# Spatial-gating statistics in two rounds with a bias table, and expert gate and up matrices laid out by tile

## The chip, the core and the metric

One core of a Trainium2 chip runs the whole program. The metric is the device time of one execution in microseconds; runs of the same kernel are compared by their median. TensorE is called PE, VectorE DVE, ScalarE ACT, GpSimd POOL and SyncE SP, as in the profile. DMAs to and from DRAM are issued by SP (plain ones) and by POOL (indirect ones); all share 16 DMA engines.

## The reference

One transformer layer on 2048 tokens of width 1024, in float32. A joint projection gives q, k, v (512 columns each) and u, vs (512 each). Attention works on a 32 x 64 grid with an 8 x 16 window. Beside it stands a spatial gating unit, which is what the first part of the change is about:

```python
def spatial_gating(u, vs, ln_g, ln_b, w_s, b_s):        # u, vs already through gelu
    n_chunks = T // SGU_CHUNK                            # chunks of 128 tokens
    vg = vs.reshape(B, T, SGU_GROUPS, SGU_GROUP_DIM)     # 8 groups of 64 channels
    vg = layer_norm(vg, ln_g, ln_b)                      # over the 64 channels of a group
    vg = vg.reshape(B, n_chunks, SGU_CHUNK, SGU_GROUPS, SGU_GROUP_DIM)
    mixed = jnp.einsum('gpq,bnqgd->bnpgd', w_s, vg) + jnp.transpose(b_s)[:, :, None]
    return u * mixed.reshape(B, T, D_SGU)
```

The two outputs are normalized, joined, projected, added to x and layer-normed. Then comes a mixture of 16 SwiGLU experts (4 groups of 4; each token goes to the best group and to two experts in it), which is what the second part is about:

```python
for e in range(MOE_EXPERTS):                             # D_EXPERT = 256
    act = jax.nn.silu(hf @ w_gate[e]) * (hf @ w_up[e])   # w_gate[e], w_up[e]: 1024 x 256
    y = y + combine[:, e:e + 1] * (act @ w_down[e])      # w_down[e]: 256 x 1024
```

A second residual and layer norm end the layer.

## The kernel before

Nearly every matrix product is made of three fp32r passes: each operand is split into a high part (a cast on ACT) and a remainder (a subtraction on DVE). The helper `split` issues the two, the helper `passes` issues the three matmuls (L132 to L134). So a matmul needs ACT and DVE to have split its operands, and these need the loads. Every line number of a split is L142 (ACT) or L143 (DVE); the tile's name tells which it is.

Four stages follow each other, with overlap at the seams. `phase_a` (to about 420 us) makes the projection and the gating unit. `phase_b` makes attention, output projection, first layer norm and routing. Its end runs together with the first experts (`Moe.ahead`, `Moe.early`). `Moe.main` works off the remaining expert jobs. A tail normalizes the last tokens.

The order of instructions on PE, ACT, DVE and POOL is the order in which the program writes them; nothing reorders them afterwards. SP's DMAs are put in order by the framework, and each engine waits with semaphores for what it reads and for buffers to come free.

`phase_a` is a sequence of blocks, `block(h, col, ...)`, one for a half of the tokens `h` and a group of 512 columns `col`. For half 0 the order is v (col 2), vs (4), k (1), u (3), q (0). For half 1 it is q, vs, u, k. A block has two sets of 4 accumulators (the first block of all: 6 and 2); for each of 8 slices of the contraction a set issues 4 x 3 matmuls of 512 columns, and then calls `pipe.step()`. At a set's end a generator (`fin_vs`, `fin_k`, ...) starts to finish the results. The pipe advances every live generator by one `yield` a step, so that a `yield` in a generator means "after the next 12 big matmuls".

`fin_vs` finishes four tiles `g` of vs, 128 tokens x 512 channels each. Counted in steps from the set's end: at 0 gelu and the sums `su`; at 1 subtraction of the mean and the sum of squares, tile by tile, with DVE and ACT in turn; at 2 the power -1/2 on POOL (tile `r`); from 4 to 7, one tile a step, the product with `r` on DVE and, on POOL, the product with the gain `gb` and the sum with the shift `bb`; at 11 the split into `vh` and `vl`; at 13 and 14 the mixing matmuls, four groups of 2 x 3 matmuls of 256 columns into PSUM tiles `mx` (two buffers), with ACT and DVE adding the bias `bs` on the way to the tile `mt`; at 15 `mt` goes to DRAM (`md`). `fin_u` reads `md` back later.

The tile `mt` has one buffer. `fin_k` uses the same buffer for half of its results, and writes them to DRAM (`kd`); the next user waits for that DMA. `fin_k` of half 0 uses two `kt` tiles first and then the two halves of `mt`. `load_sgu` loads and splits the mixing matrices `wsT` once, at the start.

The MoE works in jobs of one expert each. `load_gu(j, f)` loads a quarter of a job's gate and up matrices: a 1024 x 128 piece, 512 KB, to a tile [128 x 8 x 128] of a ring of four tiles `wr`, then splits it to `wh` and `wl`. `load_d` does it with `w_down` (rows of 4 KB) through the same ring. In DRAM an expert's gate matrix is 1024 x 256, so the piece consists of 1024 runs of 512 B. Two small jobs of the leading experts (those with `lo` above 0) load halves, two 256 KB DMAs for a tile, whose rows of 512 B lie alternately in the tile. `down` scales the result on ACT (`y`) and adds it to the tokens' rows in DRAM by an indirect DMA with accumulation (`xad<-y`, issued by POOL). `gather` fetches rows (`xg<-x1d`).

Of the kernel before, what the change touches and what calls it, by code (L numbers as in the profile page):

```python
# [8 lines left out]
F32 = mybir.dt.float32  # L9
F32R = mybir.dt.float32r  # L10
I32 = mybir.dt.int32
AF = mybir.ActivationFunctionType
OP = mybir.AluOpType
# [4 lines left out]
P = 128  # L18
T = 2048
D = 1024  # L20
KC = D // P
# [6 lines left out]
E = 16  # L28
# [12 lines left out]
NVT = 12  # L41
PSTART = 21
LATE = 14
YA = 3
YB = 2
YG = 0
FIRST = 256
WARM = 8
# [47 lines left out]
def pool(c, es, name, bufs, side="left", psum=False):  # L96
    if psum:
        return es.enter_context(c.tc.tile_pool(name=name, bufs=bufs, space=PSUM, reuse_waits="tile"))
    return es.enter_context(c.tc.tile_pool(name=name, bufs=bufs, side=side, reuse_waits="tile"))
# [37 lines left out]
def bcast(ap, n):  # L137
    return bass.AP(tensor=ap.tensor, offset=ap.offset, ap=[[0, P], [1, n]])


def split(nc, hi, lo, src):
    nc.scalar.copy(hi, src)  # L142
    nc.vector.tensor_tensor(lo, src, hi.bitcast(F32), op=OP.subtract)  # L143


def phase_a(c, xT, w_in, wsT, bsT, sg_g, sg_b):
    tc, nc = c.tc, c.nc
# [7 lines left out]
    with ExitStack() as es:  # L155
# [3 lines left out]
        sp = pool(c, es, "sp", 1, "right")  # L159
        ev = pool(c, es, "ev", 2, "right")  # L160
        acc = pool(c, es, "acc", 6, psum=True)
        mx = pool(c, es, "mx", 2, psum=True)
# [40 lines left out]
        gb = sp.tile([P, 512], F32, name="gb")  # L203
        bb = sp.tile([P, 512], F32, name="bb")
        bs = sp.tile([P, 8], F32, name="bs")
# [4 lines left out]
        def load_sgu():  # L210
            nt, ng = 3 * E * S // P, 8 * T // P
            z = sp.tile([P, nt + ng], I32, name="mt")
            zt, zg = z[:, 0:nt].rearrange("p (r o) -> p r o", o=3), z[:, nt:].rearrange("p (r o) -> p r o", o=2)
            nc.vector.memset(z, 0)
            for v in (zt, zg):
                nc.vector.memset(v[:, :, 1:2], NONE)
            nc.vector.memset(zg[:, :, 0:1], T)
            nc.sync.dma_start(c.table[:, :].rearrange("(p c) o -> p c o", p=P), zt)
            nc.sync.dma_start(c.gtok[:, :].rearrange("(p c) o -> p c o", p=P), zg)
            nc.sync.dma_start(gb, bcast(sg_g, 512))  # L220
            nc.sync.dma_start(bb, bcast(sg_b, 512))
            nc.sync.dma_start(bs, bsT)
            wsr = sp.tile([P, 8, P], F32, name="mt")
            nc.sync.dma_start(wsr, wsT)
            yield
            yield
            split(nc, wsh[:, :, :], wsl[:, :, :], wsr[:, :, :])
            yield pipe

        def fin_v(h, units, ps):  # L230
# [10 lines left out]
        def fin_vs(h, units, ps):  # L241
            q = (h * 8 + units[0]) // 4
            g = [ev.tile([P, 8, 64], F32, name="g", bufs=8) for _ in range(4)]
            su = ev.tile([P, 4, 8], F32, name="su")
            for n in range(4):
                nc.scalar.activation(g[n], ps[n], AF.Gelu_apprx_tanh)
                nc.vector.tensor_reduce(su[:, n], g[n], axis=AX.X, op=OP.add)
            yield
            va = ev.tile([P, 4, 8], F32, name="va")
            for n in range(4):  # L250
                nc.vector.scalar_tensor_tensor(g[n], su[:, n, :, None].to_broadcast([P, 8, 64]), -1.0 / 64, g[n],
                                               op0=OP.mult, op1=OP.add)
                sq = ev.tile([P, 8, 64], F32, name="sq")
                nc.scalar.activation(sq, g[n], AF.Square)
                nc.vector.tensor_reduce(va[:, n], sq, axis=AX.X, op=OP.add)
            nc.vector.tensor_scalar(va, va, 1.0 / 64, EPS, op0=OP.mult, op1=OP.add)  # L256
            yield
            r = ev.tile([P, 4, 8], F32, name="r")
            nc.gpsimd.tensor_tensor(r, va, mhalf[:, :, :], op=OP.pow)  # L259
            yield  # L260
            yield
            vh = sp.tile([P, 4, 512], F32R, name="vh")
            vl = sp.tile([P, 4, 512], F32R, name="vl")
            for n in range(4):
                nc.vector.tensor_tensor(g[n], g[n], r[:, n, :, None].to_broadcast([P, 8, 64]), op=OP.mult)
                f = g[n][:, :, :].rearrange("p a d -> p (a d)")
                nc.gpsimd.tensor_tensor(f, f, gb, op=OP.mult)
                nc.gpsimd.tensor_tensor(f, f, bb, op=OP.add)
                yield
            for _ in range(YA):  # L270
                yield
            for n in range(4):
                f = g[n][:, :, :].rearrange("p a d -> p (a d)")
                split(nc, vh[:, n, :], vl[:, n, :], f)
            for _ in range(YB):
                yield
            mt = sp.tile([P, 4, 512], F32, name="mt")
            for g2 in range(4):
                pm = mx.tile([P, 2, 4, 64], F32, name="mx")
                for j in range(2):  # L280
                    e = g2 * 2 + j
                    s = slice(e * 64, (e + 1) * 64)
                    passes(nc, pm[:, j], wsh[:, e, :], wsl[:, e, :], vh[:, :, s], vl[:, :, s], True, True)
                for j in range(2):
                    e = g2 * 2 + j
                    s = slice(e * 64, (e + 1) * 64)
                    if j:
                        nc.vector.tensor_scalar(mt[:, :, s], pm[:, j], bs[:, e:e + 1], None, op0=OP.add)
                    else:
                        nc.scalar.activation(mt[:, :, s], pm[:, j], AF.Identity, bias=bs[:, e:e + 1])  # L290
                if g2 % 2 or YG:
                    yield
            for n in range(4):
                nc.sync.dma_start(md[q * 4 + n], mt[:, n, :])
            yield pipe
# [113 lines left out]
        x, w = [], []  # L409
# [9 lines left out]
        w, _ = block(0, 2, x, w, 4, first=True)  # L419
        w, _ = block(0, 4, x, w, 1)  # L420
        w, _ = block(0, 1, x, w, 3)
        w, _ = block(0, 3, x, w, 0)
        _, x = block(0, 0, x, w, None, nxt_x=1)
        w, _ = block(1, 0, x, w, 4)
        w, _ = block(1, 4, x, w, 3)
        w, _ = block(1, 3, x, w, 1)
        w, _ = block(1, 1, x, w, 2)
# [556 lines left out]
class Moe:  # L984
# [56 lines left out]
    def load_gu(self, pipe, j, f, lag=1):  # L1041
        nc = self.c.nc
        pos, lo, _ = JOBS[j]
        whole = j in G32
        h = self.wp.tile([P, KC, P], F32R, name="wh")
        if whole:
            r = h[:, :, :].bitcast(F32)
        else:
            r = self.raw()[:, :].rearrange("p (k f) -> p k f", k=KC)
            l = self.wp.tile([P, KC, P], F32R, name="wl")  # L1050
        m, q = divmod(f, 2)
        s = slice(m * P, (m + 1) * P)
        e = bass.ds(self.ex[pos], 1)
        if lo:
            r4 = r.rearrange("p (k o) f -> p k o f", o=2)
            for i in range(2):
                src = self.w[i][e, q * 512:(q + 1) * 512, s]
                nc.sync.dma_start(r4[:, :, i], src.rearrange("o (k p) f -> (o p) k f", p=P))
        else:
            self.issued = nc.sync.dma_start(r, self.w[q][e, :, s].rearrange("o (k p) f -> (o p) k f", p=P)).ins.name  # L1060
        self.gw[j, f] = (r, None) if whole else (h, l)
        if whole:
            return

        def rest():
            for _ in range(lag):
                yield
            split(nc, h[:, :, :], l[:, :, :], r)
            yield pipe
        pipe.add(rest())  # L1070
# [215 lines left out]
    def main(self):  # L1286
        c, tc, nc = self.c, self.c.tc, self.c.nc
        es, xg, out = self.es, self.xg, self.out
        w_gate, w_up, w_down = self.w
# [257 lines left out]
        def over(mi, i):  # L1547
            e = nc.values_load(mi[0:1, bass.ds(1 + i, 1)], engines=SP, min_val=0, max_val=E - 1)
# [4 lines left out]
            for q, w in enumerate((w_gate, w_up)):  # L1553
                t = self.xp[0].tile([P, KC, W], F32R, name=("xh", "xl")[q])
                f = t[:, :, 0:FF].bitcast(F32)
                nc.sync.dma_start(f, w[bass.ds(e, 1)].rearrange("o (k p) f -> (o p) k f", p=P))
                wts.append(f)
            wd = self.xp[1].tile([P, 2, D], F32, name="xh")
            nc.sync.dma_start(wd, w_down[bass.ds(e, 1)].rearrange("o (k p) d -> (o p) k d", p=P))
# [5 lines left out]
            for h in range(2):  # L1565
                pt = ps.tile([P, 4, P], F32, name="tp")
                for k in range(4):
                    q = (h * 4 + k) * P
# [28 lines left out]
        for j in range(2, nj):  # L1597
# [4 lines left out]
            for u in range(4):  # L1602
# [4 lines left out]
                if 4 * j + u in (LN2, LN2 + 1):  # L1607
                    r = nc.sync.dma_start(*((lng, bcast(self.ln2g, D)), (lnb, bcast(self.ln2b, D)))[4 * j + u - LN2])
# [10 lines left out]
                jn, f = divmod(4 * j + u + 5, 4)  # L1619
                if jn < nj and jn > 2:  # L1620
                    self.load_gu(pipe, jn, f, LAG)
                jn, f = divmod(4 * j + u + 1, 4)
# [7 lines left out]
                if todo and u in (CU if j < nj - 3 else CT):  # L1630
                    g, i = todo.pop(0)
# [48 lines left out]
    return mid.transpose(1, 0, 2), edge  # L1680


# [32 lines left out]
```

## Time and profile before

| | |
|---|---|
| median of 3 runs | 1328.71 us (1328.42 to 1332.13) |
| the profiled execution | 1326.6 us, its span 1324.9 us |
| mean granted PE clock | 0.972 |
| PE busy | 1230.7 us of the span |
| DVE, ACT, POOL busy | 775.6, 576.1, 452.4 us |
| moved by DMA | 261.73 MB in 193506 packets, mean 198 GB/s |

In the profile an instruction is named by its line, its engine and the tiles, output first (`mx<-vh,wsh`). "A <- B: 7.1, 2, 3.7" in a view of waits means that A waited for B 7.1 us in all, 2 times, 3.7 us the longest. In the timeline the columns are start, duration, engine, line, operation, count, and in brackets the idle time of the engine before it and what ended it. In a table of stages the last three numbers are the granted clock, the mean busy share of the 16 DMA engines (which can read a little over 1), and the GB/s that they moved. PE is busy nearly all the time, so that what the span loses is to be sought in the stretches where PE waits, or where its clock is low.

### The profile page before, as it was taken

The page shows a single profiled execution, that of the slowest core. Times are in us where ns is not written, and L with a number is a line of the kernel's source. Part 1 is how long each engine was busy: PE and PEld are TensorE (multiplying, and loading weights), DVE is VectorE, ACT ScalarE, POOL GpSimd, SP SyncE. Part 2 cuts the span into 40 slices and gives each one's busy share as a digit, 9 for nine tenths or more (in the row PEclk, how much of TensorE's full clock was granted, in tenths as well). Part 3 has the DMA queues.
Part 4 walks back from the last instruction along what each step waited for, and adds up shares of the span by engine and source line. Part 5 has one row for each costly group of instructions (what it writes and reads, how often), then busy time and mean ns, then how long its engine had stood idle before and what let it go on. Part 6 is the DMA issues. An engine that isn't in the chain of part 4 may idle for free. (4 is left out here: it accounts for less than half of the span.)

```text
span 1324.9 us, 22205 instructions
## 1 busy us (share of the span) xinstructions
PE 1230.7 (93%) x7932; PEld 1048.7 (79%) x7932; DVE 775.6 (59%) x1622; ACT 576.1 (43%) x1218; POOL 452.4 (34%) x448
## 2 busy tenths in 40 slices
PE   9998999999899997999999999988888999998980
PEld 7886888888788775888888888768777999998970
DVE  5358233424853226576676676876466568777655
ACT  5324233322342236545545445334466555555522
POOL 0046000003710013234435434442323357565475
PEclk9998999999899997999999999999999999999995
DMA  8602634450254689578668676372999999999984
GB/s 253 199 24 97 229 120 164 161 189 18 89 182 167 180 257 289 170 187 199 166 187 196 160 219 194 97 227 76 257 277 301 250 270 287 297 293 306 280 250 137
DMA packets 193506, 261.73 MB, mean 198 GB/s; under 512 B 51120, under 2 KB 126128, under 8 KB 193392
## 3 DMA queue, kind: packets, MB, share of 16 engines
q1 hardware_dynamic: 175408, 204.88, 51.6%
q0 software_dynamic: 17984, 55.40, 14.9%
q8 instruction: 63, 1.03, 0.3%
q14 instruction: 51, 0.42, 0.1%
HBM read 184.17 MB, written 80.24 MB: 200 GB/s over the span
## 5 line engine op out<-in xcount | busy, mean ns | idle before, releaser
L143 DVE TENSOR_TENSOR wl<-wr,wh 128x512 fp32r<-128x512 f32 (+1 forms) x132 | 139.4, 1063 | 96.8 <-ACT wh L142 95.6
L618 POOL TENSOR_SCALAR lg<-lg,s 128x352 f32<-128x352 f32 (+3 forms) x128 | 80.2, 626 | 289.6 <-DVE s L617 226.4
L142 ACT CAST wh<-wr 128x512 fp32r<-128x512 f32 (+1 forms) x132 | 109.6, 843 | 85.0 <-DMA wr<-w_in 41.1
L132 PE MATMUL acc<-wh,xh 128*128 128x512 f32 x320 | 125.9, 393 | 0.1
L133 PE MATMUL acc<-wl,xh 128*128 128x512 f32 x320 | 125.3, 392 | 0.2 <-DVE wl L143 0.2
L134 PE MATMUL acc<-wh,xl 128*128 128x512 f32 x320 | 125.3, 391 | 0.2
L132 PE MATMUL gu<-xh,wh 128*128 128x256 f32 (+2 forms) x416 | 124.5, 299 | 0.0
L134 PE MATMUL gu<-xh,wl 128*128 128x256 f32 (+2 forms) x416 | 124.0, 298 | 0.0
L133 PE MATMUL gu<-xl,wh 128*128 128x256 f32 (+2 forms) x416 | 123.9, 298 | 0.0
L132 PE MATMUL acc<-xh,wh 128*128 128x512 f32 x256 | 101.0, 395 | 0.7 <-DVE kt L143 0.7
L134 PE MATMUL acc<-xh,wl 128*128 128x512 f32 x256 | 100.3, 392 | 0.0
L133 PE MATMUL acc<-xl,wh 128*128 128x512 f32 x256 | 100.2, 391 | 0.0
L633 ACT COPY pT<-pt 128x384 f32<-128x384 f32 (+3 forms) x128 | 57.7, 451 | 97.4 <-PE pt L631 95.3
L605 DVE CUSTOM_DVE_ANT_0 lg<-l,tm 128x352 f32<-128x352 f32 (+3 forms) x128 | 57.8, 452 | 70.6 <-PE l L134 45.2
L259 POOL TENSOR_TENSOR r<-va,mhalf 128x32 f32<-128x32 f32 x4 | 22.5, 5636 | 212.3 <-DVE va L256 212.3
L1227 POOL DMA_INDIRECT xad<-y,ix x38 | 64.7, 1704 | 54.4 <-ACT y L1206 31.6
L1112 POOL DMA_INDIRECT xg<-x1d,ix x40 | 48.1, 1203 | 101.8 <-PE tp L1131 37.0
L132 PEld LDWEIGHTS gu<-xh,wh 128*128 128x128 f32 x416 | 79.5, 191 | 1.4
L133 PEld LDWEIGHTS gu<-xl,wh 128*128 128x128 f32 x416 | 79.2, 190 | 1.3
L134 PEld LDWEIGHTS gu<-xh,wl 128*128 128x128 f32 x416 | 79.1, 190 | 0.0
L134 PEld LDWEIGHTS acc<-wh,xl 128*128 128x128 f32 x320 | 60.3, 189 | 13.7 <-DVE xl L143 1.1
L133 PEld LDWEIGHTS acc<-wl,xh 128*128 128x128 f32 x320 | 60.4, 189 | 13.2 <-DVE wl L143 0.9
(325 smaller groups left out, 3230.2 us busy)
## 6 DMA issues: line engine op xcount, KB each, us to landing
wr<-w_in SPq DMA_DIRECT2D x72, 256.0 KB
wr<-w_down SPq DMA_DIRECT2D x34, 512.0 KB
kt<-kd SPq DMA_DIRECT2D x24, 704.0 KB
wr<-w_gate SPq DMA_DIRECT2D x30, 512.0 KB
wr<-w_up SPq DMA_DIRECT2D x30, 512.0 KB
sd<-kt SPq DMA_DIRECT2D x16, 512.0 KB
qb<-qd SPq DMA_DIRECT2D x64, 128.0 KB
sr<-sd SPq DMA_DIRECT2D x16, 512.0 KB
```

The lines of the kernel that those rows point to most:

```text
L132: nc.tensor.matmul(out, lhsT=ahi, rhs=bhi, start=first, stop=False)
L133: nc.tensor.matmul(out, lhsT=ahi, rhs=blo, start=False, stop=False)
L134: nc.tensor.matmul(out, lhsT=alo, rhs=bhi, start=False, stop=last)
L142: nc.scalar.copy(hi, src)
L143: nc.vector.tensor_tensor(lo, src, hi.bitcast(F32), op=OP.subtract)
L259: nc.gpsimd.tensor_tensor(r, va, mhalf[:, :, :], op=OP.pow)
L605: nc.vector.tensor_tensor_reduce(out=l[:, :N], in0=o.rearrange("p r c -> p (r c)"), in1=bias, scale=-1.0, scalar=3.0e38, op0=OP.add, op1=O ...
L618: nc.gpsimd.tensor_scalar(l[:, :N], l[:, :N], s, 1.0, op0=OP.mult, op1=OP.mult)
L633: nc.scalar.copy(w[0:n, 0:len(ch)], pt[0:n, 0:len(ch)])
L1112: nc.gpsimd.indirect_dma_start(out=self.xg[(self.slot[j] + s) % NXG][0:m, :], out_offset=None, in_=c.x1d[0:rows, :], in_offset=bass.Indire ...
L1227: return self.c.nc.gpsimd.indirect_dma_start(out=self.c.xad[0:rows, :], out_offset=bass.IndirectOffsetOnAxis(ap=ix, axis=0), in_=y, in_off ...
```

## The change

In `fin_vs`: the four subtractions of the mean are issued first, and then the four pairs of square and sum (two rounds). The power on POOL follows in the same step. The product with the gain `gb` moves from POOL to DVE, ahead of the product with `r`. The sum with `bb` leaves this place: since the mixing is linear, the shift enters the result as (row sum of the mixing matrix) x shift, and `load_sgu` turns `bb` into a table of that plus `bs`, once, with 8 matmuls against a column of ones and 8 operations on DVE. `mt` is then written by DVE alone, one addition of the table for each PSUM tile, where before it took two instructions, one each on ACT and DVE. Two constants of the order change: YA goes, YB becomes 4. Counted in steps: squares and power at 1, gain at 2, product with `r` and split at 5, mixing matmuls at 9 and 10, `mt` to DRAM at 11.

In the MoE: the host lays the gate and up matrices out as [expert, half of the columns, 128 rows, 8, 128], so that each of the 128 partitions of a 512 KB load reads one run of 4 KB. For the halves of the small jobs a partition reads one run of 2 KB, and the tile still receives rows of 512 B. The number of these DMAs and their order stay. A rarely taken path (`over`) follows the layout.

```diff
 def load_sgu():
     ...
             split(nc, wsh[:, :, :], wsl[:, :, :], wsr[:, :, :])
+            for _ in range(8):
+                yield
+            pr = mx.tile([P, 8], F32, name="mx")
+            for e in range(8):
+                nc.tensor.matmul(pr[:, e:e + 1], lhsT=wsr[:, e], rhs=c.ones, start=True, stop=True)
+            rs = sp.tile([P, 8], F32, name="rs")
+            nc.vector.tensor_copy(rs, pr)
+            for e in range(8):
+                s = slice(e * 64, (e + 1) * 64)
+                nc.vector.tensor_scalar(bb[:, s], bb[:, s], rs[:, e:e + 1], bs[:, e:e + 1], op0=OP.mult, op1=OP.add)
 def fin_vs(h, units, ps):
     ...
                 nc.vector.scalar_tensor_tensor(g[n], su[:, n, :, None].to_broadcast([P, 8, 64]), -1.0 / 64, g[n],
                                                op0=OP.mult, op1=OP.add)
+            for n in range(4):
                 sq = ev.tile([P, 8, 64], F32, name="sq")
                 nc.scalar.activation(sq, g[n], AF.Square)
                 nc.vector.tensor_reduce(va[:, n], sq, axis=AX.X, op=OP.add)
             nc.vector.tensor_scalar(va, va, 1.0 / 64, EPS, op0=OP.mult, op1=OP.add)
-            yield
             r = ev.tile([P, 4, 8], F32, name="r")
             nc.gpsimd.tensor_tensor(r, va, mhalf[:, :, :], op=OP.pow)
+            yield
+            for n in range(4):
+                f = g[n][:, :, :].rearrange("p a d -> p (a d)")
+                nc.vector.tensor_tensor(f, f, gb, op=OP.mult)
+            yield
             yield
             yield
     ...
                 nc.vector.tensor_tensor(g[n], g[n], r[:, n, :, None].to_broadcast([P, 8, 64]), op=OP.mult)
                 f = g[n][:, :, :].rearrange("p a d -> p (a d)")
-                nc.gpsimd.tensor_tensor(f, f, gb, op=OP.mult)
-                nc.gpsimd.tensor_tensor(f, f, bb, op=OP.add)
-                yield
-            for _ in range(YA):
-                yield
+                nc.scalar.copy(vh[:, n, :], f)
             for n in range(4):
                 f = g[n][:, :, :].rearrange("p a d -> p (a d)")
-                split(nc, vh[:, n, :], vl[:, n, :], f)
+                nc.vector.tensor_tensor(vl[:, n, :], f, vh[:, n, :].bitcast(F32), op=OP.subtract)
             for _ in range(YB):
                 yield
     ...
-                    if j:
-                        nc.vector.tensor_scalar(mt[:, :, s], pm[:, j], bs[:, e:e + 1], None, op0=OP.add)
-                    else:
-                        nc.scalar.activation(mt[:, :, s], pm[:, j], AF.Identity, bias=bs[:, e:e + 1])
+                add = bb[:, s].rearrange("p (j d) -> p j d", j=2)[:, :, None, :].to_broadcast([P, 2, 4, 64])
+                nc.vector.tensor_tensor(mt[:, :, s].rearrange("p n (j d) -> p j n d", j=2), pm, add, op=OP.add)
 def load_gu(self, pipe, j, f, lag=1):
     ...
-                src = self.w[i][e, q * 512:(q + 1) * 512, s]
-                nc.sync.dma_start(r4[:, :, i], src.rearrange("o (k p) f -> (o p) k f", p=P))
+                src = self.w[i][e, m, :, q * 4:(q + 1) * 4, :]
+                nc.sync.dma_start(r4[:, :, i], src.rearrange("o p k f -> (o p) k f"))
         else:
-            self.issued = nc.sync.dma_start(r, self.w[q][e, :, s].rearrange("o (k p) f -> (o p) k f", p=P)).ins.name
+            self.issued = nc.sync.dma_start(r, self.w[q][e, m].rearrange("o p k f -> (o p) k f")).ins.name
+def by_tile(w):
+    return w.reshape(E, KC, P, 2, P).transpose(0, 3, 2, 1, 4)
```

How the instructions stand on DVE, half 0, from the statistics of the second vs set on (`su` to `va`; `vl` here is still that of the first set), before:

```order
L247 TENSOR_REDUCE su<-g 128x8 x4
L251 SCALAR_TENSOR_TENSOR g<-su,g 128x512
L255 TENSOR_REDUCE va<-sq 128x8
L251 SCALAR_TENSOR_TENSOR g<-su,g 128x512
L255 TENSOR_REDUCE va<-sq 128x8
L251 SCALAR_TENSOR_TENSOR g<-su,g 128x512
L255 TENSOR_REDUCE va<-sq 128x8
L251 SCALAR_TENSOR_TENSOR g<-su,g 128x512
L255 TENSOR_REDUCE va<-sq 128x8
L256 TENSOR_SCALAR va<-va 128x32
L143 TENSOR_TENSOR vl<-g,vh 128x512 x4
```

And the same engine now, from the gain of the first set (L272) to the power's input of the second (L266):

```order
L272 TENSOR_TENSOR g<-g,gb 128x512 x4
L142 TENSOR_TENSOR wl<-wr,wh 128x512
L279 TENSOR_TENSOR g<-g,r 128x512 x4
L284 TENSOR_TENSOR vl<-g,vh 128x512 x4
L142 TENSOR_TENSOR wl<-wr,wh 128x512 x3
L256 TENSOR_REDUCE su<-g 128x8 x4
L296 TENSOR_TENSOR mt<-mx,bb 128x2x4x64 x2
L260 SCALAR_TENSOR_TENSOR g<-su,g 128x512 x4
L265 TENSOR_REDUCE va<-sq 128x8 x4
L266 TENSOR_SCALAR va<-va 128x32
```

The first set's `vl` moved from behind the second set's statistics to before them.

The second place is where `fin_k` of half 0 has filled `mt` and the second vs set wants it for its mixing result. DVE before:

```order
L143 TENSOR_TENSOR kt<-acc,kt 128x512 x2
L143 TENSOR_TENSOR mt<-acc,mt 128x512 x2
L143 TENSOR_TENSOR vl<-g,vh 128x512 x4
L143 TENSOR_TENSOR wl<-wr,wh 128x512
L288 TENSOR_SCALAR mt<-mx,bs 128x4x64 x2
L143 TENSOR_TENSOR wl<-wr,wh 128x512
L288 TENSOR_SCALAR mt<-mx,bs 128x4x64 x2
```

DVE now:

```order
L284 TENSOR_TENSOR vl<-g,vh 128x512 x4
L142 TENSOR_TENSOR wl<-wr,wh 128x512 x3
L142 TENSOR_TENSOR kt<-acc,kt 128x512 x2
L142 TENSOR_TENSOR mt<-acc,mt 128x512 x2
L296 TENSOR_TENSOR mt<-mx,bb 128x2x4x64 x4
L142 TENSOR_TENSOR wl<-wr,wh 128x512 x4
```

The write of `mt` by the mixing results now follows directly on `fin_k`'s write of `mt`; on PE its matmuls stand one step (12 big matmuls) behind the end of `fin_k`'s set, where it was five. SP's queue at that place, now:

```order
L308 DMA m<-md_140 128x512
L189 DMA wr<-w_in 128x512 x3
L349 DMA kd_129<-kt 256x1x512 x2
L349 DMA kd_130<-mt 256x1x512 x2
L300 DMA md_141<-mt 128x512
L300 DMA md_142<-mt 128x512
```

Before, the four loads of `m` stood behind the four writes of `kd`, and one load of `wr` ahead of them; now the loads of `m` and three loads of `wr` stand ahead.

More of the change, by code (lines that the diff above doesn't have):

```diff
@@ L43 @@
 LATE = 14
-YA = 3
-YB = 2
+YB = 4
 YG = 0
@@ L283, in fin_vs @@
                     passes(nc, pm[:, j], wsh[:, e, :], wsl[:, e, :], vh[:, :, s], vl[:, :, s], True, True)
-                for j in range(2):
-                    e = g2 * 2 + j
-                    s = slice(e * 64, (e + 1) * 64)
-                    if j:
-                        nc.vector.tensor_scalar(mt[:, :, s], pm[:, j], bs[:, e:e + 1], None, op0=OP.add)
-                    else:
-                        nc.scalar.activation(mt[:, :, s], pm[:, j], AF.Identity, bias=bs[:, e:e + 1])
+                s = slice(g2 * 128, g2 * 128 + 128)
+                add = bb[:, s].rearrange("p (j d) -> p j d", j=2)[:, :, None, :].to_broadcast([P, 2, 4, 64])
+                nc.vector.tensor_tensor(mt[:, :, s].rearrange("p n (j d) -> p j n d", j=2), pm, add, op=OP.add)
                 if g2 % 2 or YG:
@@ L1051, in load_gu @@
         m, q = divmod(f, 2)
-        s = slice(m * P, (m + 1) * P)
         e = bass.ds(self.ex[pos], 1)
@@ L1555, in over @@
                 f = t[:, :, 0:FF].bitcast(F32)
-                nc.sync.dma_start(f, w[bass.ds(e, 1)].rearrange("o (k p) f -> (o p) k f", p=P))
+                for m in range(2):
+                    src = w[bass.ds(e, 1), m].rearrange("o p k f -> (o p) k f")
+                    nc.sync.dma_start(f[:, :, m * P:(m + 1) * P], src)
                 wts.append(f)
@@ L1700 @@
         b_r=np.concatenate([i["router_group_b"][0], i["router_expert_b"][0]]),
-        w_gate=i["expert_w_gate"][0], w_up=i["expert_w_up"][0], w_down=i["expert_w_down"][0],
+        w_gate=by_tile(i["expert_w_gate"][0]), w_up=by_tile(i["expert_w_up"][0]), w_down=i["expert_w_down"][0],
         ln2g=i["ln2_g"][0], ln2b=i["ln2_b"][0],
```

## The prediction

> **What bounds the kernel now.** I read the page first, then the waits of PE, then PE's timeline around the longest waits, then windows on both sides of them.
>
> ```profile
> PE 1230.7 (93%) x7932; PEld 1048.7 (79%) x7932; DVE 775.6 (59%) x1622; ACT 576.1 (43%) x1218; POOL 452.4 (34%) x448
> ...
> PE mx L132 <- ACT vh L142: 7.1, 2, 3.7
> ...
> PE mx L133 <- DVE vl L143: 1.5, 2, 0.7
> ...
> PE mx L325 <- DVE mt L288: 0.7, 2, 0.4
> PE acc L132 <- DVE kt L143: 0.7, 1, 0.7
> ```
>
> PE is busy 1230.7 of 1324.9 us, so a change gains only where PE waits or where its clock is low. Four of these waits belong to the gating unit (`vh`, `vl`, `mt`, `kt`). In the timeline of PE they stand here:
>
> ```profile
> 107.31 0.39 PE L134 MATMUL acc<-xh,wl 128*128 128x512 f32 x1
> 111.43 0.58 PE L132 MATMUL mx<-vh,wsh 128*128 128x256 f32 x1 [3.73 <-ACT vh L142]
> ...
> 119.19 0.28 PE L132 MATMUL mx<-vh,wsh 128*128 128x256 f32 x1
> 119.31 0.28 PE L133 MATMUL mx<-vl,wsh 128*128 128x256 f32 x1
> ...
> 120.62 0.39 PE L132 MATMUL acc<-xh,wh 128*128 128x512 f32 x1
> 120.85 0.40 PE L133 MATMUL acc<-xl,wh 128*128 128x512 f32 x1
> ...
> 343.33 0.39 PE L134 MATMUL acc<-wh,xl 128*128 128x512 f32 x1
> ...
> 356.23 0.39 PE L132 MATMUL acc<-wh,xh 128*128 128x512 f32 x1
> ...
> 110.00:115.00 5.00, 2.82 (x11) 2.53 (x12) 2.67 (x6) 2.38 (x5) 4.68 (x1) 0.59 0.02 3
> ```
>
> At full clock a matmul of 512 columns follows its neighbour after 0.23 us (120.62 to 120.85), one of 256 columns after 0.12 (119.19 to 119.31). The window reads: length, busy PE, PEld, DVE, ACT, POOL, then granted clock, DMA share, GB/s. Around the 3.73-us wait the clock falls to 0.59, and the small matmuls of this stretch take longer than 0.12 us, so the wait costs about twice its length.
>
> Why `vh` is late: the groups by line, and where the first vs set starts.
>
> ```profile
> L267 POOL TENSOR_TENSOR g<-g,gb 128x512 f32<-128x512 f32 x16 | 27.5, 1718 | 3.4 <-DVE g L265 3.4
> L268 POOL TENSOR_TENSOR g<-g,bb 128x512 f32<-128x512 f32 x16 | 25.0, 1562 | 1.3
> L259 POOL TENSOR_TENSOR r<-va,mhalf 128x32 f32<-128x32 f32 x4 | 22.5, 5636 | 212.3 <-DVE va L256 212.3
> L265 DVE TENSOR_TENSOR g<-g,r 128x512 f32<-128x512 f32 x16 | 20.8, 1299 | 18.1 <-POOL r L259 18.1
> L251 DVE SCALAR_TENSOR_TENSOR g<-su,g 128x512 f32<-128x512 f32 x16 | 11.1, 694 | 0.0
> ...
> 70.34 2.64 ACT L246 ACTIVATE g<-acc 128x512 f32<-128x512 f32 x4 [7.95 <-PE acc L134]
> ...
> 524.61 0.61 PE L881 MATMUL l<-ones,sq 128*128 128x1 f32 x4
> ```
>
> POOL takes 3.28 us a tile for gain and shift. The DVE product with `r` beside it has a mean of 1299 ns, where a DVE operation of the same size takes 694 with POOL idle. So the second set's statistics, and the splits behind them, start late on an in-order DVE.
>
> **The change part by part.**
>
> *a and b, the two stalls.* From 107.54 (107.31 + 0.23) PE has 12 small, 12 big and 12 small matmuls before the one at 120.62: 1.4 + 2.8 + 1.4 = 5.6 us, which would end at 113.2. It starts 7.4 us later. In half 1, 343.56 + 5.6 = 349.2 against 356.23: 7.0 us. After the change the mixing matmuls come 4 steps earlier, or 48 x 0.23 = 11 us: PE wants `vh` at about 96.5. DVE's path now: gelu from 70.34 and sums to about 73.7 (2.64 for four, the sums close behind), four subtractions 2.8 to 76.5, squares and sums 2.7 to 79.2, power 5.6 to 85, with the four gains (2.8) beside it, product with `r` 2.8 to 87.8, and the last `vl` at 90.6. That leaves 6 us, more than the operations that PE's own steps order in between could use up. Both stalls go, clock loss included: -7.4 and -7.0. Bounds: 0 if the product with `r` waits for its step anyway and something else is late, -14.4 in all at most. What is late next is DVE with `wl`, which now carries 16 gains more, 16 x 0.69 = 11 us over two halves, and loses 16 x 0.6 of slowing: even.
>
> *c, the two 0.7-us waits.* `mx` L325 waited for an `mt` addition that shared its buffers, and `kt` was behind the slowed DVE. The mixing leaves the steps where `fin_u` transposes, and POOL's operations are gone: -1.4, bounds 0 and -1.4.
>
> *d, the table.* Eight matmuls with one column; four of the kind take 0.61 us, so +1.2. The copy and the eight additions on DVE, about 1.5 us (each no longer than the 694 ns of a whole 512-column operation, and an eighth of it wide), stand 8 steps behind the split of the mixing matrices, where DVE, busy 59% of the span, is not what PE waits for. Nothing for them; at most +1.5.
>
> *e, a new wait.* On the trace the first k set of half 0 ends on PE at 126.1, called E. `fin_k` fills `mt` and SP writes it out. These rows show the writes of `md` and of this k set, who waited for `md`, and the rate while the k set's writes ran:
>
> ```profile
> 121.84 2.04 SPq L294 DMA_DIRECT2D md<-mt  x4
> ...
> 125.88 0.39 PE L134 MATMUL acc<-xh,wl 128*128 128x512 f32 x1
> ...
> 126.84 1.07 ACT L142 CAST mt<-acc 128x512 fp32r<-128x512 f32 x2 [1.31 <-DMA md<-mt]
> ...
> 128.32 1.28 SPq L343 DMA_DIRECT2D kd<-kt  x2
> 129.71 2.15 SPq L343 DMA_DIRECT2D kd<-mt  x2
> ...
> 132.00:136.00 4.00, 4.00 (x19) 3.31 (x18) 1.17 (x2) 0.00 (x0) 0.00 (x0) 1.00 1.01 331
> ```
>
> The mixing result now wants `mt` one step later, so DVE's addition waits for both `kd<-mt` DMAs. Queued behind it on DVE are three more additions and four `wl` splits; PE waits for the additions, since `mx` has two buffers. PE needs one back at E + 2.8 + 1.4 + 2.8 = E + 7.0, less the 0.7 us of the addition itself. Landing: 4 writes of 512 KB at 331 GB/s take 6.3 us. If DVE gets to `kt` undelayed they flow from about E - 1.3 on and, with 1.8 us from the last byte to the semaphore (my estimate: ACT, which waits for the four `md` writes of 1 MB, starts 126.84 - 121.84 = 5.0 us after their issue, 3.2 of them for the bytes at that rate), land at E + 6.8. Three `w_in` loads of 256 KB now stand ahead of them on SP's queue: 0.77 MB, 2.3 us more, E + 9.1. Before, the last transfer of that burst ended only near 140, E + 13.7, which is the upper end. So PE stalls 9.1 + 0.7 - 7.0 = +2.9 (ends: 0.5, and 7.5 plus some 3 of slow clock = +10.5). I take 2.9, as the queue's order is known. In the second vs set of half 1 the writer before is `md` itself, eight steps earlier, and no wait comes.
>
> *f, the layout.* These are the expert stage's windows, SP's first loads of gate and up, and from 945 to 1045 what ACT waited for and how many whole loads were issued:
>
> ```profile
> 859.00:863.00 4.00, 3.16 (x19) 2.41 (x18) 2.85 (x4) 0.59 (x1) 1.93 (x2) 1.00 1.08 297
> 865.00:870.00 5.00, 5.00 (x35) 3.97 (x34) 2.11 (x7) 1.31 (x2) 1.81 (x2) 1.00 1.02 397
> ...
> 945.00:1045.00 100.00, 89.39 (x570) 81.34 (x571) 61.64 (x94) 58.42 (x91) 28.26 (x21) 0.98 0.98 277
> 990.00:1000.00 10.00, 5.92 (x45) 5.24 (x44) 6.14 (x12) 5.21 (x9) 2.10 (x2) 1.00 1.00 325
> 1050.00:1200.00 150.00, 150.00 (x976) 137.15 (x976) 111.41 (x162) 83.45 (x132) 88.92 (x68) 1.00 0.97 281
> 1200.00:1290.00 90.00, 82.14 (x537) 74.01 (x536) 61.50 (x80) 40.92 (x67) 54.02 (x44) 0.98 0.93 278
> ...
> 857.42 0.39 SPq L1060 DMA_DIRECT2D wr<-w_gate  x1
> ...
> 858.63 1.83 SPq L1060 DMA_DIRECT2D wr<-w_gate  x1
> ...
> ACT wh L142 <- DMA wr<-w_up: 8.2, 8, 2.5
> ACT wh L142 <- DMA wr<-w_gate: 5.5, 3, 3.9
> ...
> wr<-w_gate SPq DMA_DIRECT2D x7, 512.0 KB
> wr<-w_up SPq DMA_DIRECT2D x7, 512.0 KB
> ```
>
> From 859 to 863 the engines move the gate and up pieces issued from 857.42 on, in 512-byte runs: 297 GB/s at full share. From 865 to 870 the traffic is mostly rows of 4 KB (1024 wide, stored to `x1d` and `xad` and gathered to `xg`): 397. A 512-KB load so takes 1.77 us of all engines now and 1.32 after, 0.45 saved. Fourteen such loads are issued in 945 to 1045, where DMA is at 0.98 and PE loses 100 - 89.4 = 10.6 us: 14 x 0.45 = 6.3 us of DMA time. Not all comes back to PE (some waits are short and run beside one another), and the loads of `w_down`, `xg` and `xad` stay: I take -4, bounds 0 and -10.6. In 1050 to 1200 PE is 100% busy in spite of a DMA share of 0.97: nothing to gain. From 1200 to 1290 PE loses 7.9 us, mostly to a chain through DVE and POOL: I take -1.5, bounds 0 and -6.3. Waits of about 2.5 us kept the clock at 1.00 there (990 to 1000), which is why e has no clock loss.
>
> The Trainium skill, page "DMA: Bandwidth & Descriptors", section "Specifications", puts the smallest transfer for line rate at 512 B, by which the runs of before are long enough already and part f is worth nothing. The rows differ: 297 against 397 GB/s. The same page, section "Why small descriptors are slow (HBM only)", counts some 3 cycles per packet; an estimate from it is 3 on 16 cycles at 512 B and 3 on 128 at 4 KB, a saving of 14% or 0.24 us a load, and the sum would be 2 to 3 us less.
>
> *Sum.* -7.4 - 7.0 - 1.4 + 1.2 + 2.9 - 4 - 1.5 = -17.2 us, from 1326.6 to 1309.4 for such a profiled execution. The median of the runs lies 2.1 us above it: **1311 us** (1.3% faster).
>
> **The rivals.**
>
> *A, the layout brings nothing.* Either the 297 GB/s are due to what else ran from 859 to 863, or PE's losses in the expert stage are not DMA's. For it: 1050 to 1200, where PE loses nothing at 0.97. Against it: ACT's 8.2 + 5.5 us of waits for exactly these loads. The sum is then -11.7, 1317 us. The first rule of the skill above would give this time too.
>
> *B, the writes of `kd` land late*, at E + 13.7, since the order of the bytes on 16 shared engines isn't SP's order. Then e is +10.5, the sum -9.6, 1319 us. For it: the share of 1.01 at 132 to 136. Against it: half of that burst now stands elsewhere.
>
> *C, slower.* The same wait decides: DVE stands still behind `mt`, so the four `wl` splits behind it starve PE in the whole k set. Gain and loss are even if e reaches 20 us (17.2 + 2.9), landing at about E + 23.5 with slow clock of 3; at E + 27 the time is some 1332. Nothing in the burst is that long: the bytes from 128.3 to 140 were all that was queued.
>
> **How the numbers follow.** Main case 0.62, A 0.20, B 0.12, C 0.04, and 0.02 for a gain spent elsewhere with no net change. What a measurement of this kernel can tell from no change is about 0.3%, 4 us. Main, A and B all end over 4 us below before, hence faster 0.91 (some of each left out for stalls that move to new places), same 0.05, slower 0.04. The range: below, f and g at their better ends (-10.6 and -6.3 against -5.5 taken) would give 1299.6; I go to 1302. Above it takes in A and B, 1317 and 1319, and a little of both: 1321.
>
> **What would show it.** In the profile after, PE's waits of `mx` for `vh` and `vl` are gone and the clock stays near 1.0 where 110 to 120 and 345 to 355 now are (a, b). POOL's busy time falls by 52.5 us (27.5 + 25.0). Around 125 to 135 DVE's `mt` waits for `kd<-mt`, and PE's `mx` for it, by about 3 us (e). In the expert stage ACT's 13.7 us of waits for gate and up loads shrink by half or more, the first loads flow near 397 GB/s, and the packets fall by some 900 a load, since 1024 runs become 128 (f). The prediction is wrong if the first comes but PE waits as long for `wl` or `mt`, or if the DMA share in 945 to 1045 stays at 0.98 with PE busy 89.

## The result, and the profile after

The changed kernel takes 1309.95 us (median of 4 runs, 1307.65 to 1312.10) against 1328.78 before (4 runs): a ratio of 0.984, 95% interval 0.982 to 0.987, 18.8 us less where 17.7 were forecast against the median first shown. The profiled execution has a span of 1309.8 us, 15.1 less than before, where the sum of the prediction gave 17.2. Traces of one and the same kernel scatter by more than these 2.1 us: further down the changed kernel, run again, left spans of 1314.8 (`e3_both`) and 1306.6 us (`e12_changed_again`). So the sizes of small gains are taken from medians, and traces serve to show what waits for what.

The page of the changed kernel: busy time by engine, the granted clock in 40 slices (the row of before stands first), and the DMA packets.

```profile
PEclk9998999999899997999999999999999999999995
...
PE 1230.8 (94%) x7948; PEld 1050.7 (80%) x7948; DVE 764.8 (58%) x1647; ACT 570.2 (44%) x1202; POOL 404.1 (31%) x416
...
PEclk9999999999999997999999999988899999999985
...
DMA packets 136161, 261.72 MB, mean 200 GB/s; under 512 B 51120, under 2 KB 60592, under 8 KB 136048
```

PE is busy as long as before (1230.7). What is gone is idle time. POOL lost 48 us of work. The packets fell by 57,345 for the same bytes, which is 64 x 896 and one more: 64 whole loads (60 into the ring `wr` and 4 straight into `wh`), and nothing from the small jobs' halves, whose rows in the tile are still 512 B. The dips of the clock in the fourth and the eleventh slice are gone. The mean clock of the whole run is not higher for it (0.971, before 0.972): slices 27 to 29, where the expert stage begins, and slice 39 now read 8, and what lowers the clock there stays open.

Gating unit. Of PE's waits between 60 and 420 us one row is left, where before there were four:

```profile
PE mx L131 <- DVE mt L296: 0.9, 1, 0.9
```

In the timelines of DVE and PE, the last `vl` of the first set and what PE does then, with a window (length, busy PE, PEld, DVE, ACT, POOL, clock, DMA share, GB/s):

```profile
86.52 2.50 DVE L279 TENSOR_TENSOR g<-g,r 128x512 f32<-128x512 f32 x4 [2.90 <-POOL r L268]
88.93 2.49 DVE L284 TENSOR_TENSOR vl<-g,vh 128x512 fp32r<-128x512 f32 x4
...
98.09 0.39 PE L133 MATMUL acc<-xh,wl 128*128 128x512 f32 x1
98.31 0.28 PE L131 MATMUL mx<-vh,wsh 128*128 128x256 f32 x1
...
97.00:100.00 3.00, 3.00 (x21) 2.72 (x20) 0.88 (x3) 0.00 (x0) 0.00 (x0) 1.00 0.00 0
345.00:350.00 5.00, 5.00 (x24) 4.14 (x23) 1.42 (x3) 2.40 (x4) 0.00 (x0) 1.00 0.50 157
```

`vl` ends at 91.4; the mixing matmuls start at 98.31, close behind the `acc` of 98.09, so 6.9 us of cover are left. One product with `r` takes 0.69 us (median of 16) where it took 1.3, now that POOL does no elementwise work beside it; with the gain back on POOL (`e5_gain_pool` below) it takes 1.5.

How far PE is ahead shows where the same matmul starts in both kernels: the first one after the second mixing of the kernel before (before, then after), and the first product of the attention stage (before, then after).

```profile
146.39 0.39 PE L132 MATMUL acc<-xh,wh 128*128 128x512 f32 x1
...
140.63 0.39 PE L131 MATMUL acc<-xh,wh 128*128 128x512 f32 x1
...
447.81 0.33 PE L132 MATMUL l<-kt,qb 128*128 128x192 f32 x1 [1.97 <-DMA vt<-vd]
...
433.92 0.33 PE L131 MATMUL l<-kt,qb 128*128 128x192 f32 x1 [2.41 <-DMA vt<-vd]
```

It is 5.8 us ahead there, and 13.9 ahead when the attention begins. All that comes later, the expert stage included, adds only 1.2 us to this in this pair of traces.

Expert stage of the changed kernel: the stretches that answer to 945 to 1045, 1050 to 1200 and 1200 to 1290 before, and ACT's longest waits in the first of them.

```profile
933.00:1033.00 100.00, 89.95 (x574) 82.19 (x575) 61.26 (x94) 59.49 (x93) 31.23 (x21) 0.97 0.92 275
1038.00:1186.00 148.00, 148.00 (x962) 135.29 (x961) 113.23 (x167) 86.56 (x135) 90.85 (x69) 1.00 0.94 289
1186.00:1275.00 89.00, 84.55 (x547) 75.92 (x546) 59.17 (x76) 38.51 (x62) 53.61 (x41) 0.96 0.90 270
...
ACT y L1211 <- DMA xad<-y,ix: 10.1, 2, 5.1
...
ACT wh L141 <- DMA wr<-w_up: 8.7, 4, 4.3
```

DMA is less busy (0.92 for 0.98) and ACT waits 8.7 us for gate and up loads where it waited 13.7 (over the whole span 9.2 where it waited 29.1), but in the first stretch PE still loses 10.1 us of 100 (10.6 before). In the third stretch it loses 4.5 us of 89, before 7.9 of 90.

### The profile page after: what moved, and what is told of

Its sections match the earlier page's. It is cut to its first block, busy times and chain, and to the rows that moved or that the text cites. A ratio compares the mean times of both kernels' runs of the same rounds, so it can differ in the third digit from the quotient of the medians.

```text
span 1309.8 us, 22210 instructions
## 1 busy us (share of the span) xinstructions
PE 1230.8 (94%) x7948; PEld 1050.7 (80%) x7948; DVE 764.8 (58%) x1647; ACT 570.2 (44%) x1202; POOL 404.1 (31%) x416
## 5 line engine op out<-in xcount | busy, mean ns | idle before, releaser
L142 DVE TENSOR_TENSOR wl<-wr,wh 128x512 fp32r<-128x512 f32 (+1 forms) x132 | 125.5, 964 | 96.9 <-ACT wh L141 96.3
```

## The experiments

All ran beside the kernel before on the same chip; times are medians. The first four shared a chip (before: 1330.4 us), so did e5, e6, e8 and e9 (1331.4), and e7, e10, e11 and e12 (1330.0).

### The two halves of the change

`e1_gating_only` has the changed gating unit and the old layout, `e2_layout_only` the reverse, `e3_both` is the changed kernel.

> The gating part of the change, with the expert matrices as they lay before. The trace of the changed kernel is 13.5 us ahead of before when phase_a has ended. Theory (the parts add up, the rest is the layout): about 13.5 us faster, 1315. Rival A (the layout brings nothing): as fast as the whole change, about 1310. Rival L (the layout brings most): slower than 1318.

> The layout by tile alone, with the gating statistics as before. Theory: 2 to 5 us faster than before, 1324 to 1327, with ACT's waits for gate and up loads down from some 29 to under 12 us, and the rest of the gain lost to other waits (ACT's y behind xad writes, DVE's xl). Rival A: within 1.5 us of before although the waits fall. Rival L (worth 6 to 10 us): under 1322.

> The changed kernel once more, beside the two halves, so that all three are compared on one chip. If the parts add up, its gain is the sum of the two others within 2 us; expected 1310, 18 to 19 us faster. If the layout has worth only where PE comes earlier, the sum of the halves falls short of it by 3 us or more.

| | us | less than before | ratio to before, 95% interval |
|---|---|---|---|
| e1_gating_only | 1315.2 | 15.3 | 0.989 (0.986 to 0.993) |
| e2_layout_only | 1324.3 | 6.2 | 0.996 (0.993 to 0.998) |
| e3_both | 1311.1 | 19.4 | 0.985 (0.982 to 0.989) |

As expected of the parts, but for the layout alone, which gives a little more than 2 to 5 us. Both halves gain. The gains of the two add up to 21.5, 2.1 above the whole, which these intervals can't tell from it. On top of the gating part the layout is worth 4.1 us, alone 6.2. Rival A (the layout brings nothing) and rival L (it brings most) both fall.

Where the layout gains is seen at one place: the same matmul of `down` on PE in before, after, e1_gating_only and e2_layout_only, in this order.

```profile
1212.00 0.50 PE L132 MATMUL yp<-dh,a 128*128 128x512 f32 x1 [3.92 <-ACT a L142]
...
1195.44 0.50 PE L131 MATMUL yp<-dh,a 128*128 128x512 f32 x1
...
1199.85 0.80 PE L131 MATMUL yp<-dh,a 128*128 128x512 f32 x1 [3.05 <-ACT a L141]
...
1208.92 0.50 PE L132 MATMUL yp<-dh,a 128*128 128x512 f32 x1 [0.78 <-ACT a L142]
```

In all four traces with runs of 512 B (the kernel before, e1_gating_only, and further down e6_before_later and e10_whole_512) PE waits 2.8 to 3.9 us here, in the nine with the new layout 0 to 0.9.

### Which loads

`e10_whole_512` returns the 64 whole loads (the expectations count the 60 into `wr`) to runs of 512 B and keeps the new layout for the small jobs' halves; `e12_changed_again` is its measure.

```diff
-            self.issued = nc.sync.dma_start(r, self.w[q][e, m].rearrange("o p k f -> (o p) k f")).ins.name
+            self.issued = nc.sync.dma_start(r, self.w2[q][e, :, m * P:(m + 1) * P].rearrange("o (k p) f -> (o p) k f", p=P)).ins.name
```

> The changed kernel with the 60 whole gate and up loads in runs of 512 B as before; only the small jobs' halves (64 DMAs of 256 KB at most) keep the new layout with runs of 2 KB. Theory (the whole loads carry the layout's gain): as slow as the gating part alone, 4 us slower than the changed kernel, about 1315. Rival (the halves carry it, since they are read in the stretch where PE waits): within 1.5 us of the changed kernel.

> The changed kernel once more, as the measure for the three beside it on the same chip. Expected 1310 to 1311.5, 18 to 20 us faster than before.

1313.2 us against 1308.9 for the changed kernel: 4.3 us, all that the layout brings on top of the gating part. The medians point to the whole loads; the ratios to before are 0.987 (0.984 to 0.990) and 0.985 (0.982 to 0.987), which overlap, so the times alone don't settle it. That the halves' packets did not change speaks for the whole loads, and so does the trace (of the longest of its five runs, 1319.7 us): the wait at the same matmul is back, ACT's wait for `w_up` is 27.3 us (before 17.1, after 8.7), and where the first three loads flow alone, the rate is 294 GB/s; in the changed kernel's trace it is 372 there (second window). One such pair gives the size only roughly: 2.4 to 4.4 us behind the issue of the first load the rate is 284 to 317 in four traces with runs of 512 B, 337 to 378 in nine with 4 KB.

```profile
1202.34 0.58 PE L131 MATMUL yp<-dh,a 128*128 128x512 f32 x1 [3.82 <-ACT a L141]
...
ACT wh L141 <- DMA wr<-w_up: 27.3, 10, 7.5
...
847.00:849.00 2.00, 1.16 (x8) 0.95 (x8) 1.58 (x3) 0.34 (x1) 0.34 (x1) 1.00 1.02 294
```

```profile
847.00:849.00 2.00, 1.16 (x8) 0.73 (x7) 1.95 (x3) 0.00 (x0) 0.00 (x0) 1.00 1.01 372
```

`e8_runs_of_256` goes the other way: the whole loads in runs of 256 B.

```diff
-            self.issued = nc.sync.dma_start(r, self.w[q][e, m].rearrange("o p k f -> (o p) k f")).ins.name
+            self.issued = nc.sync.dma_start(r.rearrange("p k (o f) -> p (k o) f", o=2),
+                                            self.w2[q][e, m].rearrange("x k o p f -> (x p) (k o) f")).ins.name
```

> The changed kernel with the 60 whole gate and up loads in runs of 256 B (2048 a load, where the change has 128 of 4 KB and before 1024 of 512 B); the small jobs' halves stay as changed. If a run costs a fixed time on the DMA engines (from 310 GB/s at 512 B and 372 at 4 KB where these loads flow alone: 1.69 against 1.41 us, 0.3 ns a run over all engines), a load takes 2.0 to 2.3 us, the 60 loads 35 to 50 us more of DMA time, and with the share at 0.92 PE must wait for it: 10 us or more slower than the changed kernel. If DMA time is not what bounds the expert stage: within 4 us of it.

1338.5 us, 27 above the changed kernel of the first batch, and slower than before (ratio 1.007, 1.003 to 1.010). The stretch in which PE was never idle now has PE idle:

```profile
1038.00:1186.00 148.00, 144.22 (x910) 131.47 (x909) 100.76 (x152) 80.33 (x126) 74.80 (x59) 0.98 1.01 256
...
ACT wh L141 <- DMA wr<-w_up: 32.8, 9, 6.1
...
ACT wh L141 <- DMA wr<-w_gate: 19.7, 7, 9.1
```

In this kernel as in the changed one the 512 KB of a load lie in one piece in DRAM, so that the length of the runs, and not the place of the load, makes the difference. The pages of e10_whole_512, the changed kernel and e8_runs_of_256 (spans 1317.9, 1309.8 and 1344.9 us) give the time that the packets of SP's queue took, as a share of 16 engines' span:

```profile
q1 hardware_dynamic: 175408, 204.88, 51.6%
...
q1 hardware_dynamic: 118064, 204.88, 49.9%
...
q1 hardware_dynamic: 240944, 204.88, 54.2%
```

That is 680, 654 and 729 us of all engines. The stage turns it into time very unequally: from 4 KB to 512 B, 57,344 runs and 26 us of DMA time more cost the kernel some 4 us; from 512 B to 256 B, 65,536 runs and 49 us more cost some 23. In the last case the DMA share of the stretch is 1.01, so that no idle transfer time is left to hide it.

### Which part of the gating unit's order

`e5_gain_pool` puts the gain back on POOL, `e9_one_round` undoes the two rounds, `e6_before_later` takes the kernel before and only delays the mixing.

```diff
 e5_gain_pool, against the changed kernel
-                nc.vector.tensor_tensor(f, f, gb, op=OP.mult)
+                nc.gpsimd.tensor_tensor(f, f, gb, op=OP.mult)
 e9_one_round, against the changed kernel: square and sum stand in the loop of the subtraction
-            for n in range(4):
                 sq = ev.tile([P, 8, 64], F32, name="sq")
 e6_before_later, against the kernel before
-YB = 2
+YB = 3
```

> The changed kernel with the product with the gain back on POOL (four operations of 1.7 us behind the power; order, table and all else as changed). DVE's product with r then waits until POOL's power and gains are done, some 7 us later than now, and vl ends about as late as PE wants it (91.4 + 7 against 98.3 in the first set). Theory (only the lateness of vh and vl costs): PE's waits for them stay under 1 us each, and the time is within 2 us of the changed kernel (1310 to 1312). Rival P (POOL's work beside DVE's is the cost, wherever it stands): DVE's operations slow to 1.7 us again, PE waits over 2 us at two or more places and the clock falls: 1315 or more.

> The changed kernel with the two rounds undone: subtraction, square and sum tile by tile again, which makes the statistics about 3 us longer (four pairs at 2.05 instead of 1.28 us). Everything else as changed. Theory (cover): vl ends 6.7 to 6.9 us before PE wants it, so 3 us are hidden, and the time is the changed kernel's within 1.5 us. Rival (the two rounds are what brings the gain): 3 us or more slower than the changed kernel, with waits of PE for vh.

> The kernel before with one number changed: YB from 2 to 3, so that the mixing matmuls stand one step (12 big matmuls, 2.8 us) later, and nothing is done earlier or elsewhere. Theory (lateness): PE's two waits of about 4.5 us for vh and vl shrink to about 1.7 us each and their clock loss goes, 8 to 11 us faster than before, 1319 to 1322, less what the later writes of md add before fin_k (ACT waited 1.3 us for them, now about 4; PE would lose up to 3). Rival P (POOL's share of the work is the cost): within 2 us of before.

| | us | ratio to before, 95% interval | PE's waits in the gating unit, us |
|---|---|---|---|
| e5_gain_pool | 1318.0 | 0.991 (0.988 to 0.994) | `mt` 5.0, `kt` 2.2 |
| e9_one_round | 1314.4 | 0.988 (0.981 to 0.995) | `mt` 3.6, `kt` 0.2 |
| e6_before_later | 1329.3 | 1.000 (0.997 to 1.003) | `mt` 8.3, `vl` 1.9, `vh` 1.6, `mx` L325 1.5 |

My theory's times failed in e5 and e6, where the times came out as rival P had them (1315 or more; as slow as before); e9's interval is too wide to tell it from the changed kernel, and its trace is of the longest of its four runs. The theory's waits did not fail: in each run the wait for `vh` is gone or down to 1.6 us, and what time was lost went into another wait, for `mt`. In e6_before_later the additions that write `mt` from `mx` stand on DVE between products with `r` that POOL slows (DVE's timeline):

```profile
117.41 1.75 DVE L265 TENSOR_TENSOR g<-g,r 128x512 f32<-128x512 f32 x1
119.09 1.75 DVE L143 TENSOR_TENSOR wl<-wr,wh 128x512 fp32r<-128x512 f32 x1
120.76 0.86 DVE L288 TENSOR_SCALAR mt<-mx,bs 128x256 f32<-128x256 f32 x2
```

So delay alone moves the wait from the input of the mixing to its output, since DVE is still late. In e5_gain_pool and e9_one_round it is the wait of step e. DVE comes to `kt` 4.3 and 2.3 us later than in the changed kernel, so the writes of `kd` leave later, and DVE stands before `mt` until 134.16 and 130.80, where the changed kernel went on at 127.45 (DVE's timeline of the two):

```profile
134.16 1.29 DVE L296 TENSOR_TENSOR mt<-mx,bb 128x512 f32<-128x512 f32 x2 [8.36 <-DMA kd<-mt]
...
130.80 1.29 DVE L295 TENSOR_TENSOR mt<-mx,bb 128x512 f32<-128x512 f32 x2 [6.99 <-DMA kd<-mt]
```

### The wait for `mt`

`e4_rooms` lets `fin_k` of half 0 fill `mt` first, `e7_later` mixes two steps later, `e11_gain_pool_later` does so with the gain on POOL.

```diff
 e4_rooms, against the changed kernel
-            for u, pu, t in zip(units, ps, rooms(h == 0)):
+            for u, pu, t in zip(units, ps, rooms(False)):
 e7_later, against the changed kernel; e11_gain_pool_later, against e5_gain_pool
-YB = 4
+YB = 6
```

> The changed kernel, with one thing turned: fin_k of half 0 fills the two halves of mt first and the two kt tiles after, so that the writes kd<-mt leave first. In the changed kernel DVE waits 5.7 us for them and PE 0.9 us. Theory (the place of the writes in the queue sets this wait): DVE's wait falls by 1.3 us or more, PE's goes to 0, and the time falls by up to 0.9 us, so the same as the changed kernel within what can be told. Rival (the wait was covering another, for wl behind it on DVE): PE's loss at this place stays at 0.9.

> The changed kernel with YB 6 instead of 4: the mixing matmuls stand two steps later (5.5 us), so that the writes of kd have landed when mt is wanted (DVE waited 5.7 us for them, PE 0.9). Theory (this wait is the only loss that the change leaves in the gating unit): PE's wait of mx for mt is gone, up to 1 us faster than the changed kernel, the same within what can be told. Rival: the later mixing meets fin_u or the next fin_k, which then wait for md: 2 us or more slower.

> The gain back on POOL, as in the run of that name (7 us slower than the changed kernel, with PE waiting 5.0 us for mt and 2.2 us for kt), and YB 6 as in the run beside this one. Theory (what that run lost is the wait for the writes of kd, which DVE sends late because POOL slows it): the 5.0-us wait and its clock loss go, the 2.2 us stay, 2 to 3 us slower than the changed kernel, 1312 to 1315. Rival P (POOL's work beside DVE's costs by itself): still 6 us or more slower than the changed kernel.

e4_rooms: 1310.6 us (e3_both beside it 1311.1); no wait of PE is left between 60 and 420 us, and none of DVE for `kd` between 100 and 140. e7_later: 1310.0 (e12_changed_again 1308.9); the same. Both are the changed kernel's time within what can be told, and neither is the better version.

e11_gain_pool_later: 1307.4 us, ratio 0.984 (0.981 to 0.987), the changed kernel's time again, where e5_gain_pool had 0.991 and I expected 2 to 3 us more than the changed kernel. In its trace DVE waits for the same writes as long as before:

```profile
112.39 5.78 DVE L279 TENSOR_TENSOR g<-g,r 128x512 f32<-128x512 f32 x4 [1.34 <-POOL g L272]
...
133.14 1.29 DVE L296 TENSOR_TENSOR mt<-mx,bb 128x512 f32<-128x512 f32 x2 [8.37 <-DMA kd<-mt]
```

The wait of 8.37 us is that of e5_gain_pool (8.36), the product with `r` is slowed beside POOL's gains (5.78 us for four tiles, 2.50 in the changed kernel), and neither reaches PE, whose only wait left in the gating unit is 1.0 us for `kt`. Rival P (POOL's work beside DVE's costs by itself), which e5 and e6 had left standing, falls: that work costs where its lateness reaches PE.

## Why the prediction was right

**a and b, the two stalls (forecast -7.4 and -7.0): right.** Waits and clock dips are gone, and `vl` ended at 91.4, forecast 90.6 with 6 us of cover. (POOL's busy time fell by 48 us, forecast 52.5.) The lead of 5.8 us at 140.63 is that of a and of c's `kt` (-7.4 - 0.7) less the measured d and e (1.7 + 0.9): 5.5. Half 1 adds 13.9 - 5.8 = 8.1 us, b and c's `mx` (-7.0 - 0.7) being 7.7.

**c (-1.4): right**, both rows are gone.

**d, the table (+1.2): too small, by a row that I misread.** The profile shows each of these matmuls as two records: the four at 524.61, from which I took the price, are two matmuls of the program, and the eight of the table are 16, one after the other until the next `acc` at 46.54:

```profile
44.84 1.84 PE L231 MATMUL mx<-ones,mt 128*128 128x1 f32 x16
...
46.54 0.48 PE L131 MATMUL acc<-wh,xh 128*128 128x512 f32 x1
```

That is 1.7 us, or 0.21 a matmul.

**e, the new wait (+2.9): the mechanism right, the size too large, by the term for the loads ahead.** SP and DVE at this place, and two windows while the writes flow:

```profile
116.90 1.53 SPq L189 DMA_DIRECT2D wr<-w_in  x3
119.76 1.28 SPq L349 DMA_DIRECT2D kd<-kt  x2
121.14 2.30 SPq L349 DMA_DIRECT2D kd<-mt  x2
...
127.45 1.29 DVE L296 TENSOR_TENSOR mt<-mx,bb 128x512 f32<-128x512 f32 x2 [5.68 <-DMA kd<-mt]
...
122.00:124.00 2.00, 2.00 (x15) 1.81 (x14) 0.00 (x0) 0.62 (x1) 0.00 (x0) 1.00 1.01 379
124.00:126.00 2.00, 2.00 (x12) 1.71 (x11) 0.00 (x0) 0.00 (x0) 0.00 (x0) 1.00 1.03 384
```

The three `w_in` loads stand ahead in the queue, as the order said, but were issued 2.9 us earlier, which is longer than the 2.3 us that I added for their bytes. PE reached the mixing at 122.98, so E is 122.98 - 2.8 = 120.2, and the writes landed by E + 7.2: near the lower end (6.8), not 9.1. The writes also flowed faster, at 379 to 384 GB/s where I had taken 331. DVE waited 5.7 us, PE 0.9. Queue order gives what stands ahead, not whether it is still there. That e was the place with a sharp edge is shown by e5_gain_pool and e9_one_round: a few us of lateness ahead of it made it 5.0 and 3.6, rival B's case by another cause.

**f and g, the layout (-4 and -1.5): right in sum, wrong in place, so the sum came right by luck.** The layout brought 4.1 us (6.2 alone). The price of a load, 0.45 us of all engines, I took from 4-KB rows of other traffic. It holds roughly: by the time of the queue's packets it is 0.41 against e10_whole_512 (26 us over 64 loads), and by the two windows, 372 against 294 GB/s or 1.41 against 1.78 us, 0.37. By the Trainium skill, page "DMA: Bandwidth & Descriptors", section "Why small descriptors are slow (HBM only)", some 3 cycles of overhead per packet would make 512-B runs, by an estimate from it, about 0.86 as fast as 4-KB ones. The two windows give 0.79, the means of the four and the nine traces 0.83, so these traces can't tell the loss from that estimate. The rule of the Trainium skill, same page, section "Specifications", that 512 B is enough for line rate, doesn't hold here: both windows are at a DMA share of 1.0.

What failed is where the saving comes back. Of the 26 us of DMA time only some 4 reach PE, and the stretch from 945, where I placed 4 of the 5.5 us, gave back nearly nothing. There ACT's waits for gate and up loads shrank by 5 us, less than the half forecast, and while one wait of PE became shorter, two others grew (before 945 to 1045, then after 933 to 1033):

```profile
PE tp L1163 <- DVE xl L143: 4.1, 3, 1.6
PE pt L1131 <- DVE xl L143: 3.5, 1, 3.5
PE yp L132 <- ACT a L142: 2.5, 1, 2.5
...
PE pt L1136 <- DVE xl L142: 5.6, 1, 5.6
PE yp L131 <- ACT a L141: 4.6, 2, 2.3
PE tp L1168 <- DVE xl L142: 2.5, 3, 1.0
```

The longest of them, that of `pt`, hangs on the accumulating scatter. Rows of ACT, DVE and PE in the changed kernel:

```profile
932.48 1.27 ACT L1211 ACTIVATE y<-o,ix 128x512 f32<-128x512 f32 x2 [5.12 <-DMA xad<-y,ix]
...
934.26 1.29 DVE L142 TENSOR_TENSOR xl<-pt,xh 128x512 fp32r<-128x512 f32 x2 [5.63 <-ACT xh L141]
...
935.00 0.48 PE L1136 MATMUL pt<-ident,xg 64*128 64x64 f32 x2 [5.63 <-DVE xl L142]
```

ACT waits until `y` has been scattered, the casts of `xh` stand behind it, DVE's `xl` behind these, and PE behind `xl`. The same chain stood there before, with 3.0 us of ACT's wait for the scatter. PE's wait there is 3.2 to 3.9 us in the four traces with 512-B runs; in the nine with the new layout it is 4.7 to 6.1 in seven and 2.5 in two. Why it mostly grew stays open, and that it caps the layout's gain there is read from the traces and wasn't tried.

The gain came at 1212 instead, which I had put down mostly to DVE and POOL; e1_gating_only and e10_whole_512 show that the loads decide it. Through which of the transfers they do so stays open: from 52 to 6 us ahead of that matmul ACT waits for loads and for the scatter 12.5 us in all in the kernel before, 10.2 in e1, 9.5 in e10 and 1.5 in the changed kernel, and in each with another share of the two.

## What to carry to other kernels

A late producer can cost PE more than the wait: here 8.6 us of waits for `vh` and `vl` cost 14.4, the rest in slow clock (0.59 around the first). So price a stall by when the next work starts at full rate, not by the idle time in brackets. When work is moved earlier to end a wait, look for the buffer that its output needs: here a third of the gain hung on whether four DMA writes had landed when one tile was wanted again (e5_gain_pool), and two steps more of distance made it insensitive (e11_gain_pool_later). When transfers are made cheaper, expect their gain where PE waits for them last, which the waits of the engine behind them do not tell: follow the chain from PE backwards.

## What was not expected of the hardware

The price of short runs was steeply unequal in its effect: 512-B runs in place of 4-KB ones cost this kernel about 4 us, 256-B ones about 27. Two-input DVE operations of 512 columns took 1.5 to 1.8 us beside POOL's elementwise work and 0.7 without it, yet as e11_gain_pool_later shows the kernel paid nothing for it once two steps more lay between.
